# Side-by-side first chunks, deferred few-token transposes and a full-height retention block in a two-layer encoder trunk

## The chip, the cores and the metric

The kernel runs on one core of a Trainium2 chip. The metric is the device time of one execution in microseconds (us), the median of the runs shown.

## The reference

One inference step of a streaming encoder trunk of two layers, d_model 1024. There are 16 meta tokens, 256 frames of a new stream and 32 frames of a running one; they share all weights, so the kernel treats them as T = 304 columns of one matrix. A layer is: a SwiGLU FFN (width 2816) with a residual and a layer norm; one product with w_in that gives the inputs of three branches and their gates; the branches; a gated sum, w_out and a layer norm; a second FFN and a layer norm.

```python
h = layer_norm(ALPHA * h + 0.5 * swiglu(h, up1, down1), ln_g[0], ln_b[0])
q_r, k_r, v_r, g_r, q_s, k_s, v_s, u, gates = split(h @ w_in)
o_r, s_new = retention(rotary(q_r), rotary(k_r) * DK_RET ** -0.5, v_r, s0)   # 4 heads, 128 x 256
o_s = stick_breaking(q_s, concat(past_k, k_s), concat(past_v, v_s))          # 8 heads of 128
o_p, buf_new = pool_mixer(u, pool_buf, pool_w, pool_scale)
mix = (sigmoid(gates) * einsum('btnc,ncd->btnd', [o_r, o_s, o_p], w_branch)).sum(2) @ w_out
h = layer_norm(ALPHA * h + mix, ln_g[1], ln_b[1])
h = layer_norm(ALPHA * h + 0.5 * swiglu(h, up2, down2), ln_g[2], ln_b[2])
```

Everything is f32. The outputs are the trunk's result, the new keys and values, the new retention state and the pooling buffer.

## The kernel before, in words

Activations lie transposed: channels on 128 partitions, the 304 tokens along the free dimension. A product is a row of chunks; a chunk is one 128 x 304 output in a PSUM bank, summed over k input tiles (8 for an input of 1024 channels, 22 behind the FFN's width). The precision of f32 is kept with fp32r matmuls on split operands: each number is a rounded part (hi) and a rest (lo), and `dense` (L335) issues three matmuls for each weight tile, hi by hi (L343), hi by lo (L344) and lo by hi (L345).

The weights come in blocks of 8 tiles (512 KB) in the order in which `weight_tiles` (L47) lists them. For each block SP issues a load (`fetch`, L227), ACT writes the rounded part whi (L202 under `act`) and DVE the rest wlo (L196 under `tt`); `wtile` keeps three blocks ahead of PE.

The order of all work is written out by hand. `dense` first calls `pump`, which advances the generators in `side` by a step, then `tick`, which counts down deferred pieces (`defer(n, fn)` runs n chunks later), and after its matmuls `advance`, which moves the epilogues in `stages` on. What is emitted earlier stands earlier in its engine's queue, and every queue runs in order.

**Norm** (L400 and below). While the chunks of the product ahead of a norm come in, `chunk` and `centre` add the residual, subtract a pivot and write un, the centred input times the gain, as unh and unl. The product behind the norm starts on un at once: for its first 16 chunks the division by the standard deviation is done on the output. A generator `run` (L475) splits the sums, runs the mean matmuls (L393, L394, tiles st_hi and st_lo), works out the standard deviation (rs_y; ACT and DVE), and then writes the normalized input hn tile by tile. It is put into `side` behind chunk 0; its second step, with the mean matmuls, is emitted ahead of chunk 2, the third (`newton`) ahead of chunk 3. From then on pending chunks are emptied, two per chunk: `value` (L527) copies two columns (cc) and scales on DVE (un, L199), then multiplies on POOL (un, L196). The pool psd of PSUM has 3 banks (pd), psa 5 (pa); chunks 3 to 5 go to pa. Five norms have a product behind them: two feed w_in, two (behind w_out) feed ffn2, one feeds layer 1's ffn1.

**The first product** (layer 0's ffn1, `Plain`, L558) has no norm. `begin` (L244) loads the first weight block and the input x in three parts each, in turn, and splits them.

**Few tokens.** The attention branch works on two groups of 4 heads. `v_transposes` (L624) turns the values of two heads with four PE transposes (L628); with the last pair, POOL gathers the 16 meta and 32 running tokens into a tile few (L633), PE transposes it twice (L636) and DVE copies the result to vm (L637), all emitted in a row. `sb_group` reads vm later.

**Retention.** The 304 tokens are three blocks of keys: 128, 128 and 48. `vr_transposes` (L787) transposes the values, `ret_head` (L801) does one head: scores (L806 to L808), transposes of the keys (L809 to L811), masks, then for each half e the products L840 to L845, of which L845 is the third block on 48 partitions, and L850, the new state, on 48 partitions too. The masks decc and ksc are tables.

Of the kernel before, what the change touches and what calls it, by code (L numbers as in the profile page):

```python
# [16 lines left out]
KD = 8  # L17
# [19 lines left out]
TPD = 8  # L37
# [6 lines left out]

def weight_tiles(l):  # L47
# [6 lines left out]
    for j in range(KF):  # L54
        chunk("ffn1_up", (l,), range(KD), j)
        chunk("ffn1_up", (l,), range(KD), KF + j)
    for n in range(KD):
        chunk("ffn1_down", (l,), range(KF), n)
    for g in range(2):
        for base in (32, 40, 24):  # L60
            for i in range(4):
                chunk("w_in", (l,), range(KD), base + 4 * g + i)
# [18 lines left out]
    for j in range(KF):  # L81
        chunk("ffn2_up", (l,), range(KD), j)
        chunk("ffn2_up", (l,), range(KD), KF + j)
# [10 lines left out]
def tables():  # L94
# [35 lines left out]
    for h in range(HR):  # L130
# [4 lines left out]
        decc[:48, h] = np.where((dc >= 0) & same, np.exp(lg[h] * np.maximum(dc, 0)), 0)  # L135
# [3 lines left out]
        ksc[:16, h, 2] = np.exp(lg[h] * (15.0 - np.arange(16)))  # L139
        ksc[16:48, h, 3] = np.exp(lg[h] * (31.0 - np.arange(32)))  # L140
# [22 lines left out]
def trunk(ctx, tc, xT, wts, kc_d, vc_d, s0_d, sp_d, vec_d, tab_d, y_d, kv_d, ret_d, pool_d):  # L163
# [80 lines left out]
    def begin(h, hl):  # L244
        A.preload_act_table_set(SIG_SET)
        raws[0] = wraw.tile([128, TPD * 128], F32, tag="raw", name="raw")
        parts = ((0, 2), (2, 4), (4, 8))
        for a, b in parts:
            q = slice(a % 4, a % 4 + b - a)
            SP.dma_start(out=raws[0][:, a * 128:b * 128], in_=wts[0, :, a * 128:b * 128])  # L250
            SP.dma_start(out=h[a // 4][:, q, 0:T], in_=xT[a // 4, :, q])
        for i in range(1, NRAW):
            fetch(i)
        hi = whl.tile([128, TPB * 128], F32R, tag="hi", name="whi", bufs=AHEAD + 2)
        lo = whl.tile([128, TPB * 128], F32R, tag="lo", name="wlo", bufs=AHEAD + 1)
        for a, b in parts:
            p = slice(a * 128, b * 128)
            act(hi[:, p], raws[0][:, p])
            tt(V, lo[:, p], raws[0][:, p], hi[:, p].bitcast(F32), ALU.subtract)
            for n in range(a, b):  # L260
                split(hl[0][n // 4][:, n % 4, 0:T], hl[1][n // 4][:, n % 4, 0:T], h[n // 4][:, n % 4, 0:T])
        his[0], los[0] = hi, lo
        raws.pop(0)
        fetch(NRAW)
        prep_hi(1)
        state["blk"] = 1
# [81 lines left out]

    def hl_list(hl, n):
# [50 lines left out]
    class Norm:  # L400
        def __init__(self, h, c0, gi, final=False):
# [5 lines left out]
            self.pending, self.used = [], 0  # L407
# [127 lines left out]


        def dense(self, c0, epi):
            i = self.used
            self.used += 1
            if i >= UCHUNKS:  # L540
                ps = dense(hl_list(self.hl, KD), c0)
                start(epi(ps, None))
                return
# [609 lines left out]
```

## Time and profile before

| what | value |
|---|---|
| median of 3 runs | 1816.94 us (1815.91 to 1817.55) |
| profiled execution, its own time | 1817.93 us |
| its span, first to last instruction | 1816.2 us |
| mean granted TensorE clock | 0.992 |
| PE busy | 97% of the span |
| DVE, ACT, POOL busy | 62%, 47%, 29% |
| weights read | 491 blocks of 512 KB |

How to read it: PE is TensorE's matmul row, PEld its weight loads, which run beside matmuls. A row of a timeline gives the start in us, the duration in us, engine, line, operation, output and inputs by the program's names, shape, count, and in brackets the idle time before it with what ended it. Matmuls are pipelined, so a row's duration is longer than the distance to the next one; the distance between starts is what a matmul costs. The granted clock is a share of 2.4 GHz.

### The profile page before, as it was taken

To read this page: it belongs to the slowest core of one execution; us is meant where nothing else is said; L and a number is where in the kernel's file an instruction comes from. 1 tells how busy PE (TensorE), PEld (TensorE's weight loads), DVE (VectorE), ACT (ScalarE), POOL (GpSimd) and SP (SyncE) were. 2 spreads that over 40 slices of the span, in tenths; PEclk is the share of its full clock that TensorE was granted. 3 is DMA by queue.
4 is the path that set the end of the run, shared out by engine and by line. 5 is a ranking of instruction groups with operands and counts; after the bars stand their busy time and mean duration, and the time that the engine had idled before them with its cause. 6 is when DMAs were issued, how large, how long until landed. Compare 5 with 4: busy or idle time off the path is not lost.

```text
span 1816.2 us, 31692 instructions
## 1 busy us (share of the span) xinstructions
PE 1767.2 (97%) x12704; PEld 1739.1 (96%) x12704; DVE 1134.5 (62%) x1631; ACT 845.3 (47%) x1345; POOL 535.3 (29%) x554
## 2 busy tenths in 40 slices
PE   8999999999999999999999999999999999999996
PEld 8999999999999999999999999999999899999996
DVE  5444576655685568844588445767556855797444
ACT  4434465443544445544455434554445444555432
POOL 1111344210162235511345113442101622372112
PEclk9999999999999999999999999999999999999998
DMA  7545465343335544545445545653444455445551
GB/s 263 165 151 160 154 208 193 119 141 123 132 118 182 158 144 130 164 156 162 152 132 164 157 154 160 202 199 119 151 127 133 125 190 163 150 129 185 163 164 49
DMA packets 81764, 281.19 MB, mean 155 GB/s; under 512 B 8656, under 2 KB 15696, under 8 KB 81488
## 3 DMA queue, kind: packets, MB, share of 16 engines
q1 hardware_dynamic: 80976, 277.06, 48.4%
q8 instruction: 100, 1.64, 0.4%
q0 software_dynamic: 640, 2.10, 0.3%
q14 instruction: 48, 0.39, 0.1%
HBM read 270.62 MB, written 8.50 MB: 154 GB/s over the span
## 4 chain that ended last, share of the span: by engine, by line
PE 84%; DVE 9%; POOL 4%; issue 2%; ACT 1%; DMA 1%; SPq 0%; ACTq 0%; DVEq 0%; POOLq 0%
PE pd L343 26%; PE pd L344 26%; PE pd L345 26%; DVE wlo L196 3%; DVE sg L199 2%; POOL x L196 1%; POOL pw L196 1%; DVE sl L196 1%; PE pa L345 1%; PE pa L344 1%; PE pa L343 1%; POOL un L196 1%; DVE unl L199 1%; PE pa L840 1%; DVE x L196 0%
## 5 line engine op out<-in xcount | busy, mean ns | idle before, releaser
L196 DVE TENSOR_TENSOR wlo<-raw,whi 128x1024 fp32r<-128x1024 f32 (+1 forms) x494 | 641.3, 1300 | 171.7 <-PE pd L345 96.2
L202 ACT ACTIVATE whi<-raw 128x1024 fp32r<-128x1024 f32 (+1 forms) x494 | 515.9, 1049 | 188.3 <-PE pd L344 133.6
L343 PE MATMUL pd<-hnh,whi 128*128 128x304 f32 (+1 forms) x1696 | 517.9, 305 | 4.3 <-ACT pu L202 4.2
L344 PE MATMUL pd<-hnl,whi 128*128 128x304 f32 (+1 forms) x1696 | 510.5, 301 | 0.0
L345 PE MATMUL pd<-hnh,wlo 128*128 128x304 f32 (+1 forms) x1696 | 510.2, 301 | 0.0
L343 PEld LDWEIGHTS pd<-hnh,whi 128*128 128x128 f32 x1696 | 320.5, 189 | 7.3 <-ACT pu L202 4.7
L344 PEld LDWEIGHTS pd<-hnl,whi 128*128 128x128 f32 x1696 | 320.8, 189 | 0.6
L345 PEld LDWEIGHTS pd<-hnh,wlo 128*128 128x128 f32 x1696 | 320.4, 189 | 0.0
L344 PE MATMUL pd<-sl,whi 128*128 128x304 f32 (+1 forms) x704 | 212.2, 301 | 0.0
L343 PE MATMUL pd<-sh,whi 128*128 128x304 f32 (+1 forms) x704 | 212.1, 301 | 0.0
L345 PE MATMUL pd<-sh,wlo 128*128 128x304 f32 (+1 forms) x704 | 211.9, 301 | 0.0
L196 DVE TENSOR_TENSOR sg<-sg,pd 128x304 f32<-128x304 f32 (+1 forms) x128 | 59.7, 467 | 198.3 <-ACT sg L202 125.5
L196 POOL TENSOR_TENSOR sl<-sg,sh 128x304 fp32r<-128x304 f32 (+1 forms) x64 | 76.9, 1202 | 346.1 <-ACT sh L202 346.1
L343 PE MATMUL pd<-unh,whi 128*128 128x306 f32 (+1 forms) x520 | 161.4, 310 | 9.1 <-DVE un L199 7.3
L344 PE MATMUL pd<-unl,whi 128*128 128x306 f32 (+1 forms) x520 | 160.0, 308 | 2.0 <-DVE unl L199 2.0
L345 PE MATMUL pd<-unh,wlo 128*128 128x306 f32 (+1 forms) x520 | 159.4, 307 | 0.0
L196 POOL TENSOR_TENSOR un<-un,rs_y 128x304 f32<-128x304 f32 (+1 forms) x80 | 87.9, 1106 | 184.3 <-DVE cc L530 119.1
L202 ACT ACTIVATE sh<-sg 128x304 fp32r<-128x304 f32 (+1 forms) x88 | 39.9, 456 | 202.9 <-DVE sg L196 145.0
L345 PEld LDWEIGHTS pd<-sh,wlo 128*128 128x128 f32 x704 | 132.9, 189 | 0.0
L343 PEld LDWEIGHTS pd<-sh,whi 128*128 128x128 f32 x704 | 132.8, 189 | 0.0
L344 PEld LDWEIGHTS pd<-sl,whi 128*128 128x128 f32 x704 | 132.8, 189 | 0.0
L343 PE MATMUL pd<-xh,whi 128*128 128x304 f32 x352 | 109.1, 310 | 6.1 <-ACT xh L202 6.1
(283 smaller groups left out, 3196.8 us busy)
## 6 DMA issues: line engine op xcount, KB each, us to landing
raw<-in_wts SPq DMA_DIRECT2D x491, 512.0 KB, 3.6
kc<-in_kc SPq DMA_DIRECT2D x8, 512.0 KB, 5.6
vc<-in_vc SPq DMA_DIRECT2D x8, 512.0 KB, 5.4
out_kv<-ks SPq DMA_DIRECT2D x4, 608.0 KB, 5.6
out_kv<-vs SPq DMA_DIRECT2D x4, 608.0 KB, 6.5
out_ret<-st POOLq DMA_DIRECT2D x8, 256.0 KB, 2.3
tab<-in_tab SPq DMA_DIRECT2D x1, 1753.0 KB, 9.1
out_y<-x SPq DMA_DIRECT2D x4, 288.0 KB, 2.3
```

The source lines that it names most:

```text
L196: e.tensor_tensor(out=out, in0=a, in1=b, op=op)
L199: e.scalar_tensor_tensor(out=out, in0=a, scalar=s, in1=b, op0=op0, op1=op1)
L202: A.activation(out, in_, f, **kw)
L343: PE.matmul(o, wh, xh[:, c0:c1], start=(k == 0), stop=False)
L344: PE.matmul(o, wh, xl[:, c0:c1], start=False, stop=False)
L345: PE.matmul(o, wl, xh[:, c0:c1], start=False, stop=(k == n - 1))
L840: PE.matmul(po[:, a], w[:, s], x[:, a], start=(i == 0), stop=False)
```

## The change

`weight_tiles`, `Plain.dense` and `Norm.dense` interleave the first chunks of a product: behind a norm 3 chunks first run over input tiles 0 to 5 one after the other, then over tiles 6 and 7; in the first product 2 chunks run over tiles 0 and 1, 2 and 3, 4 to 7. A new `dense_lead` issues them; the norm's generator takes its first step between the two parts and its second, with the mean matmuls, behind the three chunks. `begin` loads and splits the first two weight blocks in parts in that order. The copies into few go to ACT, and the two transposes with the copy to vm are deferred by three more chunks. The third retention block takes the last 128 tokens instead of the last 48; the tables are zero for the 80 that the second block already has. The diff, cut where the same replacement of 48 rows by 128 repeats:

```diff
@@ -42,6 +42,9 @@
 LN_SET, SIG_SET = "natural_log_exp_and_others", "sigmoid_and_others"
 NT_W = 7
 
+LEAD, LEAD_K = 3, (range(0, 6), range(6, KD))
+FIRST, FIRST_K = 2, (range(0, 2), range(2, 4), range(4, KD))
+
 
 
 def weight_tiles(l):
@@ -51,15 +54,19 @@
         for k in ks:
             out.append((name, pre, k, n))
 
-    for j in range(KF):
-        chunk("ffn1_up", (l,), range(KD), j)
-        chunk("ffn1_up", (l,), range(KD), KF + j)
+    def product(name, ns, first=False):
+        n, parts = (FIRST, FIRST_K) if first else (LEAD, LEAD_K)
+        for ks in parts:
+            for i in ns[:n]:
+                chunk(name, (l,), ks, i)
+        for i in ns[n:]:
+            chunk(name, (l,), range(KD), i)
+
+    ups = [i for j in range(KF) for i in (j, KF + j)]
+    product("ffn1_up", ups, l == 0)
     for n in range(KD):
         chunk("ffn1_down", (l,), range(KF), n)
-    for g in range(2):
-        for base in (32, 40, 24):
-            for i in range(4):
-                chunk("w_in", (l,), range(KD), base + 4 * g + i)
+    product("w_in", [base + 4 * g + i for g in range(2) for base in (32, 40, 24) for i in range(4)])
     for n in range(24):
         chunk("w_in", (l,), range(KD), n)
     for n in range(KD):
@@ -78,9 +85,7 @@
         chunk("w_branch", (l, 2), range(KD), n)
     for n in range(KD):
         chunk("w_out", (l,), range(KD), n)
-    for j in range(KF):
-        chunk("ffn2_up", (l,), range(KD), j)
-        chunk("ffn2_up", (l,), range(KD), KF + j)
+    product("ffn2_up", ups)
     for n in range(KD):
         chunk("ffn2_down", (l,), range(KF), n)
     return out
@@ -132,12 +137,12 @@
         dec[:, h] = np.where(dl >= 0, np.exp(lg[h] * np.maximum(dl, 0)), 0)
         dc = np.arange(48)[None, :] - np.arange(48)[:, None]
         same = (np.arange(48)[None, :] < 16) == (np.arange(48)[:, None] < 16)
-        decc[:48, h] = np.where((dc >= 0) & same, np.exp(lg[h] * np.maximum(dc, 0)), 0)
+        decc[80:, h] = np.where((dc >= 0) & same, np.exp(lg[h] * np.maximum(dc, 0)), 0)
...
@@ -243,27 +248,30 @@
 
     def begin(h, hl):
         A.preload_act_table_set(SIG_SET)
-        raws[0] = wraw.tile([128, TPD * 128], F32, tag="raw", name="raw")
-        parts = ((0, 2), (2, 4), (4, 8))
-        for a, b in parts:
-            q = slice(a % 4, a % 4 + b - a)
-            SP.dma_start(out=raws[0][:, a * 128:b * 128], in_=wts[0, :, a * 128:b * 128])
-            SP.dma_start(out=h[a // 4][:, q, 0:T], in_=xT[a // 4, :, q])
-        for i in range(1, NRAW):
+        for i in range(2):
+            raws[i] = wraw.tile([128, TPD * 128], F32, tag="raw", name="raw")
+        parts = ((0, 0, 2, (0, 2)), (0, 2, 4, None), (0, 4, 8, (2, 4)), (1, 0, 4, (4, 6)), (1, 4, 8, (6, 8)))
+        for i, a, b, x in parts:
+            SP.dma_start(out=raws[i][:, a * 128:b * 128], in_=wts[i, :, a * 128:b * 128])
+            if x:
+                q = slice(x[0] % 4, x[0] % 4 + 2)
+                SP.dma_start(out=h[x[0] // 4][:, q, 0:T], in_=xT[x[0] // 4, :, q])
+        for i in range(2, NRAW):
             fetch(i)
-        hi = whl.tile([128, TPB * 128], F32R, tag="hi", name="whi", bufs=AHEAD + 2)
-        lo = whl.tile([128, TPB * 128], F32R, tag="lo", name="wlo", bufs=AHEAD + 1)
-        for a, b in parts:
+        for i in range(2):
+            his[i] = whl.tile([128, TPB * 128], F32R, tag="hi", name="whi", bufs=AHEAD + 2)
+            los[i] = whl.tile([128, TPB * 128], F32R, tag="lo", name="wlo", bufs=AHEAD + 1)
+        for i, a, b, x in parts:
             p = slice(a * 128, b * 128)
-            act(hi[:, p], raws[0][:, p])
-            tt(V, lo[:, p], raws[0][:, p], hi[:, p].bitcast(F32), ALU.subtract)
-            for n in range(a, b):
+            act(his[i][:, p], raws[i][:, p])
+            tt(V, los[i][:, p], raws[i][:, p], his[i][:, p].bitcast(F32), ALU.subtract)
+            for n in range(*(x or (0, 0))):
                 split(hl[0][n // 4][:, n % 4, 0:T], hl[1][n // 4][:, n % 4, 0:T], h[n // 4][:, n % 4, 0:T])
-        his[0], los[0] = hi, lo
-        raws.pop(0)
-        fetch(NRAW)
-        prep_hi(1)
-        state["blk"] = 1
+        for i in range(2):
+            raws.pop(i)
+            fetch(NRAW + i)
+        prep_hi(2)
+        state["blk"] = 2
 
     def wtile():
         p = state["pos"]
@@ -346,6 +354,27 @@
         advance()
         return ps
 
+
+    def dense_lead(specs, parts, between=None):
+        out = []
+        for p, ks in enumerate(parts):
+            for i, (xs, c0, c1, pool) in enumerate(specs):
+                if p == 0:
+                    pump(2)
+                    tick()
+                    out.append(pa() if pool == "a" else psd.tile([128, 512], F32, tag="d", name="pd"))
+                o = out[i][:, c0:c1]
+                for k in ks:
+                    (xh, xl), (wh, wl) = xs[k], wtile()
+                    PE.matmul(o, wh, xh[:, c0:c1], start=(k == 0), stop=False)
+                    PE.matmul(o, wh, xl[:, c0:c1], start=False, stop=False)
+                    PE.matmul(o, wl, xh[:, c0:c1], start=False, stop=(k == len(xs) - 1))
+                if p == len(parts) - 1:
+                    advance()
+            if p == 0 and between:
+                between()
+        return out
+
     def hl_list(hl, n):
         return [(hl[0][k // 4][:, k % 4], hl[1][k // 4][:, k % 4]) for k in range(n)]
 
@@ -404,7 +433,7 @@
             self.gb = vec[:, gi * 16:gi * 16 + 16].rearrange("p (n t) -> p n t", t=2)
             self.s, self.q, self.ready = t304("lns"), t304("lnq"), False
             A.preload_act_table_set(LN_SET)
-            self.pending, self.used = [], 0
+            self.pending, self.lead, self.used = [], [], 0
             if not final:
                 self.un = pair_r("un")
                 for i in range(2):
@@ -533,6 +562,10 @@
             tt(G, t[:, c], t[:, c], self.rs[:, c], ALU.mult)
             return t, cc[:, 1:2]
 
+        def begin(self):
+            self.gen = self.run()
+            next(self.gen)
+
 
         def dense(self, c0, epi):
             i = self.used
@@ -541,10 +574,15 @@
                 ps = dense(hl_list(self.hl, KD), c0)
                 start(epi(ps, None))
                 return
+            if i < LEAD:
+                self.lead.append((c0, epi))
+                if i == LEAD - 1:
+                    specs = [(hl_list(self.un, KD), o, TW, None) for o, _ in self.lead]
+                    self.pending += [(p, o, e) for p, (o, e) in zip(dense_lead(specs, LEAD_K, self.begin), self.lead)]
+                    next(self.gen)
+                    side.insert(0, self.gen)
+                return
             ps = dense(hl_list(self.un, KD), c0, TW, pool="a" if i in (3, 4, 5) else None)
-            if i == 0:
-                self.gen = self.run()
-                side.insert(0, self.gen)
             self.pending.append((ps, c0, epi))
             if i == UCHUNKS - 1:
                 while self.gen in side:
@@ -557,9 +595,16 @@
 
     class Plain:
         def __init__(self, hl):
-            self.hl = hl
+            self.hl, self.lead = hl, []
 
         def dense(self, c0, epi):
+            if len(self.lead) < FIRST:
+                self.lead.append(epi)
+                if len(self.lead) == FIRST:
+                    specs = [(hl_list(self.hl, KD), c0, T, None)] * FIRST
+                    for p, e in zip(dense_lead(specs, FIRST_K), self.lead):
+                        start(e(p, None))
+                return
             start(epi(dense(hl_list(self.hl, KD), c0), None))
 
     def ffn(h, src, gi, c0, final):
@@ -630,11 +675,14 @@
         if i == 3:
             few = t304("few")[:, 0:256]
             for k, o in enumerate((0, 272)):
-                G.tensor_copy(few[:, k * 128:k * 128 + 128].rearrange("p (a b) -> p a b", a=4), vs[:, :, o:o + 32])
-            p = pa()
-            for k in range(2):
-                PE.transpose(p[:, k * 128:k * 128 + 128], few[:, k * 128:k * 128 + 128], ident)
-            V.tensor_copy(vm, p[:, 0:256])
+                act(few[:, k * 128:k * 128 + 128].rearrange("p (a b) -> p a b", a=4), vs[:, :, o:o + 32])
+            defer(3, lambda: few_transposes(few, vm))
+
+    def few_transposes(few, vm):
+        p = pa()
+        for k in range(2):
+            PE.transpose(p[:, k * 128:k * 128 + 128], few[:, k * 128:k * 128 + 128], ident)
+        V.tensor_copy(vm, p[:, 0:256])
 
 
 
@@ -789,35 +837,36 @@
         src = vr[j // 4][:, j % 4]
         PE.transpose(p[:, 0:128], src[:, 0:128], ident)
         PE.transpose(p[:, 128:256], src[:, 128:256], ident)
-        PE.transpose(p[0:48, 256:384], src[:, 256:304], ident)
+        PE.transpose(p[:, 256:384], src[:, T - 128:T], ident)
         h, e = j // 2, j % 2
...
     def ret_head(l, c0, h, qr, kr, vt, s0, od, var):
         vh, vl = [flat(vt[k][h // 2])[:, (h % 2) * 512:(h % 2) * 512 + 512] for k in range(2)]
-        vc = flat(vt[2])[0:48, h * 256:h * 256 + 256]
+        vc = flat(vt[2])[:, h * 256:h * 256 + 256]
         p, pk = pa(), pa()
         q, k = qr[:, h], kr[:, h]
         PE.matmul(p[:, c0:272], k[:, 0:128], q[:, c0:272], start=True, stop=True)
         PE.matmul(p[:, 272:416], k[:, 128:256], q[:, 128:272], start=True, stop=True)
-        PE.matmul(p[0:48, 416:464], k[:, 256:304], q[:, 256:304], start=True, stop=True)
+        PE.matmul(p[:, 416:464], k[:, T - 128:T], q[:, 256:304], start=True, stop=True)
...
@@ -842,12 +891,12 @@
                       start=False, stop=False)
             for w, x in ((vh, xbh), (vh, xbl), (vl, xbh)):
                 PE.matmul(po[:, 128:400], w[:, s2], x, start=False, stop=False)
-            PE.matmul(po[:, 256:432], vc[:, s], xc[0:48, 0:176], start=False, stop=True)
+            PE.matmul(po[:, 256:432], vc[:, s], xc[:, 0:176], start=False, stop=True)
             act(o[:, 2 * (h % 2) + e, c0:272], po[:, c0:272])
             act(o[:, 2 * (h % 2) + e, 272:304], po[:, 400:432])
             V.tensor_copy(st[:, s], po[:, 272:400])
         pst = pa()
-        PE.matmul(pst[:, 0:256], xc[0:48, 176:304], vc, start=True, stop=True)
+        PE.matmul(pst[:, 0:256], xc[:, 176:304], vc, start=True, stop=True)
         stt(V, st[:, 256:512], flat(s0)[:, h * 256:h * 256 + 256], GAMMA32[h], pst[:, 0:256], ALU.mult, ALU.add)
         G.dma_start(out=ret_d[l, h], in_=st[:, 0:512])
         c = slice(c0, T)
```

## Rows read from the trace of the kernel before

**Rows 1.** The page: busy time of TensorE, and the chain by engine.

```profile
PE 1767.2 (97%) x12704; PEld 1739.1 (96%) x12704; DVE 1134.5 (62%) x1631; ACT 845.3 (47%) x1345; POOL 535.3 (29%) x554
...
PE 84%; DVE 9%; POOL 4%; issue 2%; ACT 1%; DMA 1%; SPq 0%; ACTq 0%; DVEq 0%; POOLq 0%
```

**Rows 2.** Waits of PE: releaser, us in total, times, longest us.

```profile
PE pd L343 <- DVE un L199: 7.3, 12, 1.0
PE pa L636 <- POOL few L633: 7.3, 2, 3.8
PE pd L343 <- ACT xh L202: 6.1, 3, 4.8
...
PE pd L344 <- DVE unl L199: 2.0, 4, 1.0
...
PE pd L343 <- ACT unh L202: 1.6, 2, 0.8
```

**Rows 3.** Timeline of PE around layer 0's few-token transposes.

```profile
269.96 0.60 PE L628 MATMUL pa<-tab,vs 128*128 128x128 f32 x4
...
274.42 0.51 PE L343 MATMUL pd<-unh,whi 128*128 128x306 f32 x1
...
278.00 0.30 PE L345 MATMUL pd<-unh,wlo 128*128 128x306 f32 x1
```

**Rows 4.** Stretches: us, busy PE, PEld, DVE, ACT, POOL, granted clock, DMA, GB/s.

```profile
249.20:274.30 25.10, 21.57 (x155) 21.25 (x153) 17.80 (x28) 17.93 (x30) 24.36 (x24) 1.00 0.56 172
274.50:277.95 3.45, 3.45 (x15) 3.45 (x15) 1.56 (x2) 0.82 (x2) 0.00 (x0) 0.51 0.23 21
690.95:694.40 3.45, 3.45 (x16) 3.45 (x15) 2.45 (x4) 1.38 (x3) 0.00 (x0) 0.51 0.45 141
700.15:747.07 46.92, 44.52 (x308) 43.56 (x307) 45.01 (x65) 25.30 (x42) 34.11 (x30) 1.00 0.39 124
927.38:974.31 46.93, 44.35 (x307) 43.26 (x306) 45.18 (x65) 25.36 (x42) 34.11 (x30) 1.00 0.39 123
```

**Rows 5.** Timeline of PE behind the norm between the layers.

```profile
915.73 0.30 PE L343 MATMUL pd<-unh,whi 128*128 128x306 f32 x1
...
922.50 0.30 PE L393 MATMUL pa<-st_hi,onesr 128*128 128x304 f32 x1
```

**Rows 6.** Timeline of PE and DVE behind layer 0's w_out norm.

```profile
684.57 0.30 PE L343 MATMUL pd<-unh,whi 128*128 128x306 f32 x1
689.43 0.54 DVE L199 SCALAR_TENSOR_TENSOR unl<-x,vec,unh 128x304 fp32r<-128x304 f32 x1
695.34 0.30 PE L393 MATMUL pa<-st_hi,onesr 128*128 128x304 f32 x1
700.67 1.22 DVE L196 TENSOR_TENSOR wlo<-raw,whi 128x1024 fp32r<-128x1024 f32 x1 [0.52 <-ACT whi L202]
706.39 1.66 DVE L196 TENSOR_TENSOR wlo<-raw,whi 128x1024 fp32r<-128x1024 f32 x1 [0.58 <-PE pa L345]
```

**Rows 7.** Timeline of PE and PEld: f32 at full height, weight loads, a retention head.

```profile
296.54 0.62 PE L653 MATMUL pa<-ks,qs 128*128 128x272 f32 x2
...
297.14 0.30 PE L344 MATMUL pd<-hnl,whi 128*128 128x304 f32 x1
...
393.03 0.14 PEld L791 LDWEIGHTS pa<-tab,vr 128*128 128x128 f32 x1
393.13 0.10 PEld L792 LDWEIGHTS pa<-tab,vr 128*48 128x48 f32 x1
...
442.22 0.29 PE L844 MATMUL pa<-xbl,vtrh 128*128 128x272 f32 x1
442.35 0.29 PE L844 MATMUL pa<-xbh,vtrl 128*128 128x272 f32 x1
...
443.35 0.34 PE L840 MATMUL pa<-xal,vtrh 128*128 128x400 f32 x1
443.53 0.34 PE L840 MATMUL pa<-xah,vtrl 128*128 128x400 f32 x1
```

More of the change, by code (lines that the diff above doesn't have):

```diff
@@ L138, in tables @@
         ksc[:, h, 1] = np.exp(lg[h] * (MP - 1.0 - 128 - m))
-        ksc[:16, h, 2] = np.exp(lg[h] * (15.0 - np.arange(16)))
-        ksc[16:48, h, 3] = np.exp(lg[h] * (31.0 - np.arange(32)))
+        ksc[80:96, h, 2] = np.exp(lg[h] * (15.0 - np.arange(16)))
+        ksc[96:, h, 3] = np.exp(lg[h] * (31.0 - np.arange(32)))
     t["dec"], t["decc"], t["qsc"], t["ksc"] = dec, decc, qsc, ksc
@@ L796, in vr_transposes @@
         split(hi, lo, p[:, 0:256].rearrange("p (a b) -> p a b", a=2))
-        V.tensor_copy(flat(vt[2])[0:48, j * 128:j * 128 + 128], p[0:48, 256:384])
+        V.tensor_copy(flat(vt[2])[:, j * 128:j * 128 + 128], p[:, 256:384])
     def ret_head(l, c0, h, qr, kr, vt, s0, od, var):
         vh, vl = [flat(vt[k][h // 2])[:, (h % 2) * 512:(h % 2) * 512 + 512] for k in range(2)]
-        vc = flat(vt[2])[0:48, h * 256:h * 256 + 256]
+        vc = flat(vt[2])[:, h * 256:h * 256 + 256]
         p, pk = pa(), pa()
@@ L807, in ret_head @@
         PE.matmul(p[:, 272:416], k[:, 128:256], q[:, 128:272], start=True, stop=True)
-        PE.matmul(p[0:48, 416:464], k[:, 256:304], q[:, 256:304], start=True, stop=True)
+        PE.matmul(p[:, 416:464], k[:, T - 128:T], q[:, 256:304], start=True, stop=True)
         PE.transpose(pk[:, 0:128], k[:, 0:128], ident)
         PE.transpose(pk[:, 128:256], k[:, 128:256], ident)
-        PE.transpose(pk[0:48, 256:384], k[:, 256:304], ident)
+        PE.transpose(pk[:, 256:384], k[:, T - 128:T], ident)
         xa, xb, xc = t560("xa")[:, 0:400], t304("xb")[:, 0:272], t304("xc")
-        dec, dcc, sc = TB("dec")[:, h], TB("decc")[0:48, h], TB("ksc")[:, h]
+        dec, dcc, sc = TB("dec")[:, h], TB("decc")[:, h], TB("ksc")[:, h]
         tt(V, xa[:, c0:272], p[:, c0:272], dec[:, c0:272], ALU.mult)
         tt(V, xb[:, 0:144], p[:, 272:416], dec[:, 0:144], ALU.mult)
-        tt(V, xc[0:48, 0:16], p[0:48, 416:432], dcc[:, 0:16], ALU.mult)
-        tt(V, xc[0:48, 144:176], p[0:48, 432:464], dcc[:, 16:48], ALU.mult)
+        tt(V, xc[:, 0:16], p[:, 416:432], dcc[:, 0:16], ALU.mult)
+        tt(V, xc[:, 144:176], p[:, 432:464], dcc[:, 16:48], ALU.mult)
         for o, i, s in ((xa[:, 272:400], pk[:, 0:128], sc[:, 0:1]), (xb[:, 144:272], pk[:, 128:256], sc[:, 1:2]),
-                        (xc[0:48, 16:144], pk[0:48, 256:384], sc[0:48, 2:3]),
-                        (xc[0:48, 176:304], pk[0:48, 256:384], sc[0:48, 3:4])):
+                        (xc[:, 16:144], pk[:, 256:384], sc[:, 2:3]),
+                        (xc[:, 176:304], pk[:, 256:384], sc[:, 3:4])):
             V.tensor_scalar(out=o, in0=i, scalar1=s, scalar2=None, op0=ALU.mult)
```

## The prediction

> **What bounds the kernel now.** I read the page's first and fourth parts, then PE's waits, then the timeline of each place the diff touches, then busy time by stretch. TensorE is busy 97% of the span and carries 84% of the chain that ended last [rows 1]: nearly every microsecond belongs to PE, and a change pays only where PE stands still, runs at the half clock, or spends more time on a matmul than its columns need. PE's waits [rows 2] name the standing still: 7.3 us in two waits for the few-token copies on POOL, 6.1 us for the first input tiles (4.8 of them before the first matmul, so 1.3 later), 3.6 us for unh and unl at the head of a product behind a norm, and 7.3 us in twelve short waits for DVE to empty a pd bank.
>
> Two things multiply a stall. After the few-token stall the granted clock is 0.51, the 1.2 GHz level, for a stretch of 3.4 us, and the same follows the stall at the norm near 688 us [rows 3, 4]. In it PE's matmuls start 0.256 us apart (274.42 to 278.00, 14 steps), against 0.141 at the 2.4 GHz level (915.73 to 922.50, 48 steps) [rows 3, 5]: one such stretch costs 14 x 0.115 = 1.6 us. And behind each norm that feeds an FFN another engine takes over: from the end of the rstd work to the first product on normalized input DVE is busy 45.0 of 46.9 us, and 45.2 of 46.9 us at the other such place [rows 4]. There PE's short stalls are only a sign that DVE sets the pace.
>
> **Few-token transposes.** Removed: POOL's two copies in front of two transposes that stand in PE's queue directly behind the four others. From the first of those four to the next dense matmul 4.46 us pass (269.96 to 274.42) [rows 3]; the six transposes need an estimated 0.6 of them, so 3.9 go. Layer 1's stall is 7.3 - 3.5 = 3.8 us instead of 3.5 [rows 2], so 4.1 go. The half-clock stretch behind each goes too: 2 x 1.6. Sum -11.2. The two other groups of values show no stall. Added: eight copies on ACT, which is busy 17.9 of 25.1 us in that stretch [rows 4]; the free 7 us cover them (some 0.3 us each), and if that cover is gone, the weight rounding queued behind them comes late, with three weight blocks in hand. The transposes and the vm copy on DVE come three products later; vm's reader, the attention group, starts later still. Bounds: -7.3 if the clock falls anyway, -11.2; I take -11.2.
>
> **Three chunks side by side behind a norm.** This has two signs. PE now runs 54 matmuls on un tiles 0 to 5 before it needs tile 6, some 7.6 us. Near 688 us the product starts at 684.57, so tiles 6 and 7 are wanted at 692.2; the last is written at 689.43 + 0.54 [rows 6]. The 3.6 us of waits at the two w_out norms [rows 2] and their half-clock stretches disappear from PE. But the time is set by DVE afterwards, and DVE starts when the mean matmuls have run. They ran behind chunk 1, at 695.34; now they stand behind chunk 2, at 684.57 + 72 x 0.141 = 694.7 [rows 6]. That is 0.65 us earlier, not four. DVE also loses two waits just behind it, 0.52 for a rounded weight block (now issued ahead of the statistics) and 0.58 for a block that PE, now ahead, has released [rows 6]: together 1.75. For layer 1, a little less by the same count, I take 1.25. Sum -3.0 instead of the 7 that PE's own stalls suggest.
>
> At the norm between the layers the sign turns. There the product starts without a wait at 915.73 and the mean matmuls run at 922.50; side by side they cannot start before 915.73 + 72 x 0.141 = 925.85 [rows 5]. The statistics are 3.35 us later, DVE is the bound behind them [rows 4], and it regains about 1 of it (the same two waits): +2.4. At the two norms that feed w_in the delay is the same, but DVE is busy only 17.8 of 25.1 us and POOL, with 24.4, sets the pace [rows 4]; PE does not wait for POOL's results there except through ACT's copy of vs ahead of the four transposes. POOL will run about 2.8 us later, which just uses up that slack: +0.5 for both. What would be late next is these transposes.
>
> Three pd banks are now filled at once; the third is wanted 36 x 0.141 = 5.1 us after the start, when DVE has read the last w_out bank, with under 1 us to spare. Bounds of the whole part: -7.5 (PE's waits and clock all won, nothing lost) to +4 (layer ends lose, w_out norms win nothing); I take -0.1, by the DVE rows.
>
> **The first product.** Two chunks side by side give 12 matmuls per pair of input tiles instead of 6. Before, 1.3 us of stalls lay behind the first matmul [rows 2]. In SP's queue the second pair of inputs now stands behind one more weight part and is issued one slot later, so it lands somewhat later; 12 matmuls at the half clock, 3 us, cover nearly all of that wait. I take 0.8 for the stalls. If PE then works without a break, the clock rises one such stretch earlier, another 1.6. Bounds -0.3 to -4.0 (two stretches); I take -2.0. The next weight blocks are fetched behind one more part each; PE reaches them at the fetch's pace at worst, which is in the upper bound.
>
> **Retention's third block.** Now 128 tokens high instead of 48 with the extra rows at zero weight: the matmuls keep their moving columns. From the last matmul before the 48-row piece to the second behind it 1.00 us pass (442.35 to 443.35) [rows 7]. Its parts at full height: 0.13 for 272 columns (442.22 to 442.35), 0.18 for 400 (443.35 to 443.53), and for the 176 columns in f32 0.30, scaled from a full-height 272-column f32 product, which with the matmul behind it took 0.60 (296.54 to 297.14), 0.46 without it [rows 7]. That is 0.61, so 0.39 is spent around a piece that is not full height. There are two per head and layer, 16 in all, every second one together with the state's product, which I count alike: -6.2, and 0.2 less because the first pair's state product waits for DVE's st anyway. The masked multiplies get no wider along a partition: nothing. The nearest row for no gain at all is the 48-column transpose, where the short side cost nothing; for a loss, weight loads: 128 columns took 0.14 and 48 columns 0.10 [rows 7], so 40 such loads cost at most 1.6. Bounds -6.5 to +1.6; I take -6.0, since the 1.00 us row is the same operation.
>
> A page speaks against this part. The Trainium skill, "TensorE: Matmul & The Clock Gate", section LDWEIGHTS, says that a weight load takes time by its columns and not by its contraction rows, columns over 1.2 GHz: an estimate by it makes 80 more columns 67 ns, for 40 loads 2.7 us, and the sum would be 1800.3. The rows differ by 40 ns, and a 128-column load lies beside a matmul, so I keep 0.
>
> **Sum.** -11.2 - 0.1 - 2.0 - 6.0 = -19.3 on the profiled execution's 1817.93 us (span 1816.2): 1798.6. The median of the three runs, 1816.94, is 1.0 lower; I predict 1798.
>
> **Rivals.** *The norm's gain stays.* PE's stalls and clock at the w_out norms are won whole (-7.5) and DVE has slack to absorb the late statistics: 1790. Against it: 45 of 46.9 us busy. Chance 0.13. *The height is not what costs.* The 0.39 belongs to the change between f32 and fp32r: 1804. Against it: the full-height row has that change and no loss. 0.15. *The wait moves.* POOL, later by 2.8 us, makes the four transposes wait for vs, or ACT the few, at both layers, and the clock falls again: the gain of 11.2 shrinks to about 3: 1806. 0.12. *Slower.* Behind an FFN's norm PE, now further ahead, meets DVE in longer stalls; from the size of the stall near 688 (1.7 us, [rows 2]: 3.6 over two layers) each drops the clock, where today's 1.0 us stalls do not. At 1.6 us each, twelve such stretches use up the gain; three norms with some ten products each offer thirty, which would give 1817 to 1830. Against it: a slow PE does not stall, so it ends by itself. 0.02. *No change*: the terms mostly fail together: 0.03.
>
> **Numbers.** The forecast, with its own variations (first product 2, clock 3), has 0.55. The range 1789 to 1807 takes in the first three rivals and the bounds of the two largest unknowns. A measurement here tells about 0.2%, 3.6 us, from no change. Faster by more 0.95, within 0.03, slower 0.02.
>
> **What would show it.** Right: no PE wait for few or unh/unl; no half-clock stretch behind the few transposes; mean matmuls near the w_out norms about 0.6 us earlier relative to the product's start and 3.35 later at the layer boundary; short pd stalls larger in sum at that boundary; pieces of 0.6 us where 1.00 stood. Wrong: a new wait of PE for vs, a half-clock stretch in the DVE-bound part, or the retention pieces still at 1.0.

## The result, and the profile after

The changed kernel takes 1796.38 us (median of 4 runs, 1795.56 to 1797.08), the kernel before beside it 1817.24 (1815.91 to 1817.76): a ratio of 0.9886, 95% interval 0.9869 to 0.9903. The prediction was 1798.

First the changed kernel's page, busy time of TensorE and the chain that ended last, then the waits of PE (us in total, times, longest), as [rows 1, 2].

```profile
span 1795.3 us, 31702 instructions
PE 1752.5 (98%) x12704; PEld 1733.4 (97%) x12704; DVE 1127.6 (63%) x1632; ACT 846.6 (47%) x1354; POOL 536.3 (30%) x546
PE 86%; DVE 8%; POOL 2%; issue 1%; DMA 1%; ACT 1%; SPq 0%; ACTq 0%; DVEq 0%; POOLq 0%
```

```profile
PE pd L351 <- DVE un L204: 12.8, 18, 1.0
PE pd L351 <- ACT pu L207: 5.6, 3, 3.2
PE pd L369 <- ACT xh L207: 4.7, 1, 4.7
PE pd L352 <- DVE rl L201: 1.8, 1, 1.8
PE pa L742 <- DVE ol L201: 1.5, 2, 0.8
PE pa L899 <- DVE st L897: 1.4, 2, 0.7
```

The waits for few, unh and unl are gone, and of the wait for xh only the one ahead of the first matmul is left. The waits for DVE's un grew from 7.3 us in twelve to 12.8 in eighteen.

Waits alone don't account for the time. I cut both timelines of PE at the same matmuls (the first of a product, or its 17th chunk) and compare the stretches. Each line of this table is one such difference, after minus before, in us:

| stretch of PE's timeline | layer 0 | layer 1 |
|---|---|---|
| first product, to the down projection | -2.84 | |
| w_in product, first to 17th chunk (few and a norm) | -5.40 | -5.36 |
| retention, first matmul to the branch behind it | -3.52 | -3.44 |
| that branch, to the pool mix | -0.26 | +1.55 |
| product behind w_out's norm, to the 17th chunk | -1.98 | -1.71 |
| product at the layer boundary, to the 17th chunk | | +1.87 |

The sum is -21.1; the end behind the last down projection's start is 0.30 longer, and the spans differ by 20.84. The rest of the program agrees to 0.1 us a stretch.

The changed kernel's timeline of PE where the few transposes now run, and in a retention head:

```profile
277.56 0.30 PE L353 MATMUL pd<-unh,wlo 128*128 128x306 f32 x1
277.69 0.38 PE L684 MATMUL pa<-tab,few 128*128 128x128 f32 x2
277.83 0.39 PE L351 MATMUL pd<-unh,whi 128*128 128x306 f32 x1
278.06 0.31 PE L352 MATMUL pd<-unl,whi 128*128 128x306 f32 x1
...
433.76 0.29 PE L893 MATMUL pa<-xbh,vtrl 128*128 128x272 f32 x1
433.89 0.46 PE L894 MATMUL pa<-xc,vtrc 128*128 128x176 f32 x2
434.06 0.47 PE L889 MATMUL pa<-xah,vtrh 128*128 128x400 f32 x1
434.37 0.34 PE L889 MATMUL pa<-xal,vtrh 128*128 128x400 f32 x1
```

No idle time stands in front of the few transposes, and they cost 0.2 us (277.56 to 278.06 is 0.50, and two steps of 0.14 are 0.28 of it). In the retention head 433.76 to 434.37 is 0.61 us where 1.00 stood [rows 7].

The same kernel's busy time by stretch (us, PE, PEld, DVE, ACT, POOL, granted clock, DMA, GB/s): the two products behind norms from where DVE sets the pace, beside those of [rows 4], and a stretch at 1429 us:

```profile
686.85:733.12 46.27, 42.28 (x289) 40.91 (x288) 45.43 (x67) 24.98 (x42) 34.37 (x30) 1.00 0.36 116
915.20:962.21 47.01, 42.72 (x295) 41.41 (x293) 46.10 (x69) 25.79 (x42) 34.29 (x30) 1.00 0.38 114
```
```profile
1429.40:1433.80 4.40, 4.40 (x23) 4.40 (x23) 3.38 (x8) 2.79 (x5) 0.68 (x1) 0.61 0.52 135
```

DVE is still busy in all but 1 us of 46 to 47. The last line is the +1.55: half clock behind a wait for rl, where the kernel before has the same wait and no half clock. Nothing in the change touches that place.

### The profile page after: what moved, and what is told of

It reads as the page before. It is cut to its first block, busy times and chain, and to the rows that moved or that the text cites. A ratio compares the mean times of both kernels' runs of the same rounds, so it can differ in the third digit from the quotient of the medians.

```text
span 1795.3 us, 31702 instructions
## 1 busy us (share of the span) xinstructions
PE 1752.5 (98%) x12704; PEld 1733.4 (97%) x12704; DVE 1127.6 (63%) x1632; ACT 846.6 (47%) x1354; POOL 536.3 (30%) x546
## 4 chain that ended last, share of the span: by engine, by line
PE 86%; DVE 8%; POOL 2%; issue 1%; DMA 1%; ACT 1%; SPq 0%; ACTq 0%; DVEq 0%; POOLq 0%
PE pd L351 26%; PE pd L352 26%; PE pd L353 26%; DVE wlo L201 3%; DVE sg L204 2%; POOL pw L201 1%; PE pd L371 1%; PE pd L369 1%; PE pd L370 1%; DVE sl L201 1%; PE pa L352 1%; PE pa L351 0%; PE pa L353 0%; PE pa L889 0%; DVE hnl L201 0%
## 5 line engine op out<-in xcount | busy, mean ns | idle before, releaser
L201 POOL TENSOR_TENSOR un<-un,rs_y 128x304 f32<-128x304 f32 (+1 forms) x80 | 95.0, 1195 | 169.4 <-DVE cc L559 122.3
L351 PE MATMUL pd<-unh,whi 128*128 128x306 f32 (+1 forms) x400 | 122.6, 306 | 12.8 <-DVE un L204 12.8
L352 PE MATMUL pd<-unl,whi 128*128 128x306 f32 (+1 forms) x400 | 120.7, 302 | 0.0
L353 PE MATMUL pd<-unh,wlo 128*128 128x306 f32 (+1 forms) x400 | 120.7, 302 | 0.0
L353 PE MATMUL pd<-xh,wlo 128*128 128x304 f32 x336 | 102.9, 306 | 0.0
```

The source lines that it names most:

```text
L201: e.tensor_tensor(out=out, in0=a, in1=b, op=op)
L351: PE.matmul(o, wh, xh[:, c0:c1], start=(k == 0), stop=False)
L352: PE.matmul(o, wh, xl[:, c0:c1], start=False, stop=False)
L353: PE.matmul(o, wl, xh[:, c0:c1], start=False, stop=(k == n - 1))
```

## The experiments

Stretch lengths below are differences on PE's timeline as above; each kernel's one profile gives them. Whole times are medians, and ratios (with a 95% interval) are to the kernel before on the same chip; where no ratio stands, the kernel ran once.

**Retention's height.** Two kernels: the third block back at 48 rows, and at 64.

```diff
-        vc = flat(vt[2])[:, h * 256:h * 256 + 256]
+        vc = flat(vt[2])[0:48, h * 256:h * 256 + 256]
-        PE.matmul(p[:, 416:464], k[:, T - 128:T], q[:, 256:304], ...)
+        PE.matmul(p[0:48, 416:464], k[:, 256:304], q[:, 256:304], ...)
...
```

For 64: `[0:64]`, `k[:, T - 64:T]`, and the tables moved to rows 16 to 63.

> The changed kernel with the third retention block back at 48 rows, all else as changed. Theory (a full-fp32 piece 48 rows high among full-height ones costs a change-over of about 0.4 us each time): the stretch from the first retention matmul to the first matmul of the branch behind it grows by 3.5 us in the first layer and 3.4 in the second (what it lost between the two kernels), so about 1803 us in all, and no other stretch changes by over 0.3 us, but for a stretch at half clock that may come or go. Rival (the gain of that stretch came from somewhere else that moved, the copies of the state on DVE or the earlier arrival of the other parts): it grows by under 1 us a layer and the time stays within 1.5 us of 1796.

> The changed kernel with the third retention block 64 rows high (the last 64 tokens, the 16 that belong to the second block weighted with zero). Theory (any piece under full height, among full-height ones, pays the change-over): as with 48 rows, +3.5 us a layer, about 1803 us. Rival (only a height that is no whole part of the array pays): the stretch stays within 0.3 us a layer of the changed kernel's, about 1796 us.

Measured: 1804.71 us (ratio 0.9924, 0.9907 to 0.9940) and 1804.72 (0.9923, 0.9908 to 0.9937). The retention stretch grew by 3.8 and 3.5 us with 48 rows, by 3.6 and 3.6 with 64; the whole time by 8 us, of which 0.5 is a later first matmul and the rest lies within the runs' spread. Timelines of PE, 48 rows, then 64:

```profile
434.31 0.29 PE L893 MATMUL pa<-xbh,vtrl 128*128 128x272 f32 x1
434.53 0.56 PE L894 MATMUL pa<-xc,vtrc 48*128 48x176 f32 x2
435.02 0.45 PE L889 MATMUL pa<-xah,vtrh 128*128 128x400 f32 x1
435.31 0.34 PE L889 MATMUL pa<-xal,vtrh 128*128 128x400 f32 x1
```
```profile
434.42 0.29 PE L893 MATMUL pa<-xbh,vtrl 128*128 128x272 f32 x1
434.63 0.56 PE L894 MATMUL pa<-xc,vtrc 64*128 64x176 f32 x2
435.12 0.45 PE L889 MATMUL pa<-xah,vtrh 128*128 128x400 f32 x1
435.42 0.34 PE L889 MATMUL pa<-xal,vtrh 128*128 128x400 f32 x1
```

Both take 1.00 us to the second matmul behind the piece, against 0.61 at full height. The loss is paid on either side of it: 0.22 instead of 0.13 from the matmul ahead, 0.49 instead of 0.17 to the one behind. So it is not the odd 48, nor the change of data type, which is the same at all three heights.

The pieces are not all of it. Compared matmul by matmul, the sixteen pieces gain 0.39 us each between the two kernels (1.00 to 0.61 alone, 1.42 to 1.04 with the state's product behind them), less 0.2 in each of two whose wait for st is longer now: 5.8 in both layers. Another 1.56 comes from the third block's scores and key transposes, whose weights are 48 columns wide before and 128 after. From one head's first score to the next head's, before, then changed:

```profile
431.77 0.62 PE L806 MATMUL pa<-qr,kr 128*128 128x272 f32 x2
433.17 0.62 PE L806 MATMUL pa<-qr,kr 128*128 128x272 f32 x2
```
```profile
423.59 0.62 PE L855 MATMUL pa<-qr,kr 128*128 128x272 f32 x2
424.79 0.62 PE L855 MATMUL pa<-qr,kr 128*128 128x272 f32 x2
```

That is 1.40 us against 1.20 (1.42 with 64 columns), and the other seven heads differ by the same 0.2. The transposes of the values, as narrow before, change by nothing. Other steps of the stretch lose 0.4.

**The few transposes.** The change did two things at once. One kernel keeps the delay and puts the copies back on POOL, one keeps ScalarE and drops the delay.

```diff
-                act(few[:, k * 128:k * 128 + 128].rearrange(...), vs[:, :, o:o + 32])
+                G.tensor_copy(few[:, k * 128:k * 128 + 128].rearrange(...), vs[:, :, o:o + 32])
```
```diff
-            defer(3, lambda: few_transposes(few, vm))
+            few_transposes(few, vm)
```

> The changed kernel with the few-token copies back on POOL, the transposes still put off by three chunks. Theory (putting off is what counts: three chunks are some 9 us, over the 3.6 us that the transposes waited for POOL): the stretch from the first to the 17th chunk of the w_in product stays at 56.3 us in the first layer and 55.7 in the second, within 0.3, no wait of a few-token transpose on PE, 1796 us. Rival (the engine of the copies counts): a wait of 1 to 3.6 us at the first transposes of each layer comes back, 1799 to 1805 us.

> The changed kernel with the few-token transposes at once behind the others again, the copies on ScalarE. Theory (putting off is what counts): PE waits for ScalarE at two to four places, 1.0 to 1.9 us each, with or without half clock behind it: the stretch of the w_in product grows by 1 to 4 us a layer, 1798 to 1804 us. Rival (the engine counts): no wait, both stretches within 0.3 us of 56.3 and 55.7, 1796 us.

Measured: 1796.99 us on POOL, both w_in stretches within 0.03 us; with the delay, the engine is worth nothing. Without the delay 1813.6 us: from the w_in product's start to the retention 8.0 and 8.3 us more in the two layers (6.7 and 7.0 of it up to the 17th chunk), more than the change had gained there. Each layer has a first wait, of 5.0 or 5.4 us, with half clock behind it, and one of 1.0 for the second group. The expectation had the sign, and at most half of the size (1 to 4 us a layer). This is ScalarE in that kernel, then PE's wait:

```profile
268.00 0.64 ACT L207 ACTIVATE x<-x,vec 128x304 f32<-128x304 f32 x1 [1.44 <-POOL x L201]
268.67 0.46 ACT L207 ACTIVATE hnh<-x 128x304 fp32r<-128x304 f32 x1
269.04 1.04 ACT L207 ACTIVATE whi<-raw 128x1024 fp32r<-128x1024 f32 x1
269.98 0.54 ACT L207 ACTIVATE qs<-un,cc 128x304 f32<-128x304 f32 x1
270.58 0.64 ACT L207 ACTIVATE x<-x,vec 128x304 f32<-128x304 f32 x1
271.26 0.46 ACT L207 ACTIVATE hnh<-x 128x304 fp32r<-128x304 f32 x1
271.62 0.58 ACT L207 ACTIVATE vt<-pa 128x512 f32<-128x512 f32 x1
272.10 0.50 ACT L207 ACTIVATE few<-vs 128x128 f32<-128x128 f32 x2
```
```profile
272.45 0.47 PE L684 MATMUL pa<-tab,few 128*128 128x128 f32 x1 [5.05 <-ACT few L207]
```

The copies take 0.5 us, but they stand behind vt's copy and six other instructions, the first of them waiting for POOL: 5.05 us of wait, against 3.53 when POOL made them inline. ScalarE's low share of busy time said nothing about its queue.

**The three chunks side by side.** Taken away everywhere, then kept only behind w_out's norms:

```diff
-            if i < LEAD:
+            if i < 0:
```
```diff
-            if i < LEAD:
+            if i < LEAD and self.gi % 3 == 1:
```

(with the order of the weight blocks to match, and the norm's own work started behind chunk 0 where there is no lead).

> The changed kernel without the three first chunks side by side behind the norms (products and the norm's own work in the order of before; the first product stays as changed). Theory (the lead brings two effects of opposite sign: behind w_out it takes the stalls at the product's start away and gives part of that back while VectorE is the bound; behind the second feed-forward block there are hardly stalls to take away, and only the loss stays): w_out's two products take 2.0 and 1.7 us longer up to their 17th chunk, the product at the layer boundary 1.9 us less, the two w_in products within 0.4 us; 1798 us. Rival (the lead is a gain everywhere and the loss at the boundary is due to the earlier arrival): the boundary stays as it is and the time is 1800 us.

> The changed kernel with the lead kept only behind the w_out norms; behind the feed-forward norms the order of before. Theory: the layer boundary gains 1.9 us back, the w_in products stay within 0.4, 1794.5 us. Rival (the boundary's loss comes from elsewhere): 1796.4.

Measured: 1794.68 us without any lead (0.9885, 0.9866 to 0.9905; one of its four runs took 1800.63) and 1794.73 with it behind w_out alone (0.9876, 0.9859 to 0.9892). The boundary gained 1.92 and 1.94, as expected, and the w_in products changed by 0.03 at most. But taking the lead from w_out's norms cost 0.43 and 0.20 us, not 2.0 and 1.7. The stalls were back at their old size (2.0 us for unl, 1.6 for unh, as in [rows 2]); the half clock behind them was not. Busy time of that kernel behind both stalls:

```profile
677.40:681.70 4.30, 4.14 (x28) 3.92 (x29) 3.82 (x6) 2.77 (x5) 0.00 (x0) 1.00 0.50 153
1561.40:1565.70 4.30, 4.15 (x29) 3.93 (x30) 3.85 (x6) 2.82 (x5) 0.00 (x0) 1.00 0.47 155
```

**When the mean runs.** The lead stays; the splits of the norm's sums go ahead of it and the statistics between its two parts. A second kernel shortens the first part at the layer boundary, with the order of the weight blocks to match.

```diff
+                    self.begin()
-                    self.pending += [... zip(dense_lead(specs, LEAD_K, self.begin), self.lead)]
-                    next(self.gen)
+                    self.pending += [... zip(dense_lead(specs, LEAD_K, lambda: next(self.gen)), self.lead)]
```
```diff
+EARLY_K = (range(0, 3), range(3, KD))
...
-dense_lead(specs, LEAD_K, lambda: next(self.gen))
+dense_lead(specs, EARLY_K if self.gi % 3 == 2 else LEAD_K, lambda: next(self.gen))
```

> The changed kernel with the splits of the norm's sums ahead of the three chunks side by side and the statistics and their matmuls between the two parts of these, in place of between and behind them. Theory (while VectorE is the bound, what decides is when its chain begins, and that is set by the mean's matmuls): they come 2.3 us earlier, so the gaps of PE in that stretch (4.0 us behind w_out, 4.3 at the boundary) shrink by about 2.3 us each: about 1789.5 us. Rival (VectorE's work, not its beginning, is what is short, for instance because the splits of the weights that were ahead of the sums now come behind them): gaps within 0.5 us of the same, 1796 us, or new waits of PE for the sums' splits between the two parts.

> As the kernel with the mean early, and at the layer boundary alone the first part of the three chunks is 3 of 8 row tiles long in place of 6, so that the mean's matmuls run behind 27 matmuls, not 54 (the splits of the sums are done 3.3 us after that product's start). Theory (behind a feed-forward block too the stretch ends later by some 0.6 us for each us that the mean's matmuls come later: 60.45 us with the mean at 10.13, 57.96 at 7.61): mean at 3.8 to 4.2, the stretch 55.5 to 56.5 us, 1.5 to 2.4 us less than with the mean early, other stretches the same but for half clock that comes or goes. Rival (below 58 us PE's own matmuls or DVE's work are the bound): 57.5 us or more.

Measured: 1793.20 us (0.9869, 0.9854 to 0.9884) and 1793.10 (0.9868, 0.9854 to 0.9881). Both in one table with the others, in us behind the product's first matmul (the mean's first matmul | the first matmul of the 17th chunk):

| kernel | w_out's norm, layer 0 | layer boundary |
|---|---|---|
| before | 10.77, 62.50 | 6.77, 58.58 |
| changed | 10.19, 60.52 | 10.13, 60.45 |
| no lead | 9.25, 60.95 | 6.78, 58.53 |
| mean early | 7.64, 59.51 | 7.61, 57.96 |
| boundary early | 7.63, 59.50 | 3.84, 58.19 |

The mean's place counts: with the lead, 2.5 us earlier ends the product 2.5 us earlier at the boundary and 1.0 behind w_out. It is not all: without the lead w_out's product ends later although its mean is earlier; PE stood still 1.5 us at its head, but that this is why was not tested. And from 7.61 to 3.84 nothing more is won: the rival of the second kernel holds. In the trace the earlier mean is worth 1.0, 2.5 and 0.5 us (w_out in layers 0 and 1 being the first and the last), where about 2.3 were expected at each; in whole times the two are the fastest kernels here, but their intervals overlap the changed kernel's.

**Less work for VectorE.** If its sum of work were the bound, giving some of it away should shorten these stretches.

```diff
-            V.tensor_copy(cc, ps[:, T:TW])
+            if self.gi % 3:
+                act(cc, ps[:, T:TW])
+            else:
+                V.tensor_copy(cc, ps[:, T:TW])
-            V.tensor_scalar(out=nm, in0=p1[:, c], scalar1=-1.0, scalar2=None, op0=ALU.mult)
+            act(nm, p1[:, c], AF.Copy, scale=-1.0)
```

> As the kernel with the boundary early, and VectorE gives work away behind the norms that feed a feed-forward block: the copies of the two bias columns (16 of 0.15 us for each norm) and the negated mean (0.47) go to ScalarE, which is busy 18.5 of 32 us there. Theory (VectorE's sum of work sets these stretches): each has 2.8 us less of it, and loses 1.5 to 2.8 us as far as PE still has gaps (3.3 us behind w_out in the first layer, 3.7 in the second, about 1 at the boundary): 4 to 6.5 us in all. Rival (what counts is the latency from one engine to the next; ScalarE's copies stand behind its rounding of weights, 1.05 us each, and VectorE waits for them): no gain, or up to 3 us more.

Measured: 1805.26 us (0.9935, 0.9921 to 0.9949), 12 more than with the boundary early; the stretches grew by 3.8, 4.6 and 3.9. The rival came, with four times its upper bound of 3 us. Groups of DVE behind w_out's norm in layer 0 (busy, mean ns | idle ahead of them), this kernel, then the mean early:

```profile
L205 DVE SCALAR_TENSOR_TENSOR un<-lnn,cc,pd 128x304 f32<-128x304 f32 x11 | 5.7, 525 | 5.1 <-ACT cc L208 5.1
```
```profile
L204 DVE SCALAR_TENSOR_TENSOR un<-lnn,cc,pd 128x304 f32<-128x304 f32 x11 | 5.8, 531 | 0.4
L559 DVE COPY cc<-pd 128x2 f32<-128x2 f32 x11 | 1.6, 148 | 0.0
```

DVE saved 1.6 us of copies and waited 5.1 for ScalarE's, some 1.0 each time. The theory of the bare sum of work falls: a copy of 0.15 us in DVE's own queue is cheaper than the hand-over that replaces it.

**The first product** in the order of before, its loads too:

```diff
-            if len(self.lead) < FIRST:
-                self.lead.append(epi)
...
             start(epi(dense(hl_list(self.hl, KD), c0), None))
...
-        parts = ((0, 0, 2, (0, 2)), (0, 2, 4, None), (0, 4, 8, (2, 4)), (1, 0, 4, (4, 6)), (1, 4, 8, (6, 8)))
+        parts = ((0, 2), (2, 4), (4, 8))
```

> The changed kernel with the very first product and its loads in the order of before. Theory (the two chunks side by side take away the stalls, and the clock gets to its full rate earlier): the first product up to the down projection is 2.8 us longer, in it 0.8 to 1.0 of stalls and 4.8 us later to the full clock at half rate, which is worth 2.4 if PE is busy in all of it; 1799 us. Rival (it is the order of the loads): half of it or less.

Measured: 1797.21 us; the first product 1.18 us longer, not 2.8. It did without the 1.16 us stall that the kernel before had. That is in the rival's range, but this kernel puts back the chunks and the loads together and can't part them. Whether that stall comes differs from one execution to the next (the second one of before has 0.64 us, at another matmul), so I count all profiles at hand: the down projection starts at 157.16 to 158.06 us of the span in eleven executions with the new order (mean 157.6), and at 160.62, 159.03 and 158.84 with the old (mean 159.5). The part is worth some 1.9 us, with three executions of the old order that differ by 1.8 among themselves. Part of it is the clock: PE's matmuls start 0.25 us apart at first and 0.14 later, and the change comes 3.3 to 5.9 us behind the first matmul in the eleven, 4.3, 7.9 and 10.3 in the three.

**Both kernels once more.**

> The changed kernel once more. Theory (whether a stall of 1 to 2 us is followed by half clock differs from one execution to the next of the same program): the stretches without stalls come out within 0.1 us, and the half clock at 1430 us is there or not, 1.5 us of difference; the first product within 1 us of 153.1. Rival (it belongs to the program): the same half-clock stretches as in its first profile.

> The kernel before once more. Theory: as for the changed kernel, so the half-clock stretches at 274, 541, 691, 1184 and 1585 us need not all be there, each worth 1.5 us, and the first product need not take 155.9 us again (with its old order in the changed kernel it took 154.3). Rival: all five are there again, none at 1450, and the first product takes 155.9 us.

Measured: 1795.71 and 1818.47 us. Busy time of the changed kernel's second profile at 1429 us, and of the second one of before behind w_out's norm and at 1449 us:

```profile
1429.40:1433.80 4.40, 4.40 (x35) 4.40 (x35) 3.38 (x8) 2.82 (x5) 0.64 (x1) 1.00 0.56 140
```
```profile
688.90:693.20 4.30, 4.14 (x28) 3.92 (x29) 3.81 (x6) 2.75 (x5) 0.00 (x0) 1.00 0.50 154
1449.20:1453.20 4.00, 4.00 (x19) 4.00 (x20) 2.98 (x7) 2.21 (x5) 0.85 (x1) 0.57 0.45 133
```

The same programs, the same stalls, and the half clock in other places: at 1429 us the changed kernel now keeps 1.00 (35 matmuls in 4.40 us, not 23); the kernel before keeps 1.00 near 689 us, where [rows 4] had 0.51, and loses it at 1449. Its product behind w_out's norm took 61.00 us in place of 62.50. Behind layer 1's wait for few its half clock lasts 6.8 us, not 3.4, and that w_in product takes 62.42 us up to its 17th chunk in place of 61.08. Stretches without stalls agree to 0.1 us. Theory confirmed.

## Why the prediction was right, and where it was not

**Few transposes**, -11.2 in the forecast together with +0.5 at w_in's norms: measured -10.76 in these two stretches. The +0.5 was wrong (no lead: 0.03 us), so the few alone are 10.8, a little under their term; beside the second profile of before they are 11.9, since the half clock lasted longer there. That the delay carries all of it was not said: I had costed the engine and the delay as one.

**Retention**, -6.0: measured -7.0, past the term's own bound of -6.5. The pieces came to 0.61 as worked out, with the state's product too; sixteen of them give 6.2, and the waits for st took 0.4 back, not 0.2. The step that failed is the one that put the rest of the third block at nothing, because a 48-column transpose had cost nothing. That row was right for the values, but the scores and key transposes, 48 columns wide as well, had cost 0.2 us a head: 1.56. The rival that blames the change of data type is refuted: the full-height piece has that change and takes 0.61, the 64-row piece has it and takes 1.00. The sentence from the Trainium skill, "TensorE: Matmul & The Clock Gate", section LDWEIGHTS, by which 40 wider weight loads would cost an estimated 2.7 us, found no counterpart: the stretch of the 24 wider loads for scores and key transposes got shorter by those 1.56 us, that of the 16 for the values stayed.

**First product**, -2.0: -2.84 in this pair of profiles, some -1.9 over all of them.

**Norms.** At the layer boundary +2.4 became +1.87: the mean came where the count put it (10.13 against 72 x 0.141 = 10.15), but 1.5 us of its delay were regained, not 1. Behind w_out the forecast of -1.75 and -1.25 looks right beside -1.98 and -1.71, and it was right for the wrong reason. I had put the gain on DVE's earlier chain and two of its waits. In layer 0 those two are gone, 1.1 us together, but a wait for ScalarE stands in their place, in time that the old order had filled with the rest of a weight block. DVE before, then in the changed kernel:

```profile
697.04 1.22 DVE L196 TENSOR_TENSOR wlo<-raw,whi 128x1024 fp32r<-128x1024 f32 x1
698.30 0.47 DVE L196 TENSOR_TENSOR rs_t<-rs_y 128x304 f32<-128x304 f32 x1
```
```profile
685.74 0.47 DVE L201 TENSOR_TENSOR rs_t<-rs_y 128x304 f32<-128x304 f32 x1 [1.17 <-ACT rs_y L207]
```

With the stalls there and no half clock behind them, the old order costs only 0.43 and 0.20 more. The other 1.5 us in each layer is the clock: at the head of such a product half clock holds the mean's matmuls back, and DVE does not make that good. In layer 0 of the kernel before, the mean and the 17th chunk came at 10.77 and 62.50 with it, and at 9.25 and 61.00 without. I had written that the clock's share would be swallowed by the DVE-bound part.

**Half clock.** The step that failed is the one that took it as a fixed follower of a stall. By place, over fourteen profiles: behind waits of 3.5 us and more for few, six of six; behind the 3.2 us wait for pu in layer 0, thirteen; behind the 1.8 us wait for rl, seven; behind the stalls at w_out's norms in the old order, three of six; behind single stalls of up to 1.03 us, none; behind a wait of 2.64 us for un, which only the kernel with less work for VectorE has, one. The three of six make the lead's expected worth there 2 x 0.5 x 1.5 + 0.6 = 2.1 us, an estimate, against 1.9 lost at the boundary: close to nothing, as the -0.1 for the whole part had it (in this pair it was -1.8). So the +1.55 in layer 1 was a draw, not an effect, and without it the two profiles would differ by 22.4. But the half clock behind layer 0's w_out norm in the first profile of before was a draw of the other sign, worth 1.5: without both they would differ by 20.9. That the whole came within 2 us of the forecast is in part luck: retention, first product and norms each gave some 1 us more than their terms, and the draw at rl took 1.5 back.

None of the rivals came: no wait for vs, no half clock in the DVE-bound part, and behind w_out only 0.6 us of gain stayed beside the clock's. What remains open is what holds the boundary's product at 58 us once the mean comes early: DVE is busy there in all but some 0.4 us of the last 29, and the one attempt to lighten it added a hand-over.

## What to carry to other kernels

When a matmul waits on a helper copy, move the reader later before you look for a faster engine: the delay gave everything here, and the other engine without it made things worse. Behind a norm ask when the statistics start, not only how much PE has to do meanwhile: matmuls set ahead of the statistics push back the engine that sets the pace (here down to a mean 7.6 us behind the product's start; earlier gave nothing). Look at short blocks among full ones, for rows and for weight columns: widened to 128 at zero weight, they took less time here than at 48 or 64. A gain read from one pair of profiles contains draws of the clock; take a second profile of the same program before giving a microsecond or two to a cause.

## What was not expected of the hardware

A matmul of 64 rows among full-height ones loses the same 0.39 us as one of 48, and a head's scores and key transposes lose 0.2 with 48 or 64 weight columns. In the first microseconds the column of the granted clock shows 1.00, and yet PE makes about half of the matmuls that it makes next; two stretches of the changed kernel, columns as before:

```profile
4.70:10.40 5.70, 5.61 (x19) 4.79 (x20) 3.67 (x8) 3.44 (x9) 0.00 (x0) 1.00 0.98 325
10.40:14.40 4.00, 4.00 (x30) 3.97 (x30) 2.98 (x6) 3.13 (x6) 0.00 (x0) 1.00 1.03 413
```

Its matmuls start 0.25 us apart in the first and 0.14 in the second. The column misleads there: the trace's record of the clock begins only at 10.36 us, with the full level, and ahead of that the view shows 1.00 for want of an entry. In all fourteen traces the spacing changes from 0.25 to 0.14 where the record begins, so by the spacing (0.256 us at that level in [rows 3, 4]) PE starts at 1.2 GHz. Last, a stall of 1.8 us (with waits of 1.0 and 1.4 in the 10 us ahead of it) is followed by half clock in half of the profiles, at 1.5 us each, and in one of two executions of the same program.
